# The last store of a mean kernel: one store of four partitions 32 apart that GpSimd awaits, or two stores of neighbouring pairs that SyncE and ScalarE issue and await

## The chip, the cores and the metric

The kernel runs on one core of one Trainium2 chip. The metric is the device time of one execution in microseconds (us); smaller is better. A profile's "span" is a little shorter than that time, since it ends with the program's last instruction and the runtime's closing part follows.

## The reference

```python
def setup_inputs():
    return {"x": np.random.randn(64, 256, 8192).astype(np.float32)}

def reference(x: np.ndarray) -> np.ndarray:
    return np.mean(x, axis=2)
```

That is 16384 rows of 8192 numbers, 536.87 MB, and one mean for each row.

## The kernel before

63 blocks of 256 rows are loaded by SyncE and summed by VectorE (the very last pieces shared with ScalarE). The last block is cut smaller and smaller, so that little work is left when its last piece lands. Its second half of 128 rows, one row per partition, ends in a column of 128 sums, one in each partition. A transpose on VectorE turns each group of 32 partitions by itself, so the results lie in four rows of 32 numbers, at partitions 0, 32, 64 and 96. One store takes these four rows.

```python
    def store_last(r):
        nc.vector.transpose(out=fin_t[r][:], in_=fin[r][:])
        return nc.sync.dma_start(out=out_last[r], in_=fin_t[r][0:P:SQ, :])
    # ... all loads and sums ...
    scaled_sum(fin[0][:, 0:1], head[:])
    st = store_last(0)
    # ...
    untracked(scaled_sum(fin[1][:, 0:1], fin_in[:, 0 : lastw + k]))._wait_ge(sem, 16)
    with tc.issue_after(st.ins):
        last_store = store_last(1)
```

At the end every engine reports by a drain (a semaphore counts the reports), GpSimd waits for the four reports, clears the kernel's semaphores, and awaits the last store, which no other engine waits for.

```python
    with nc.body("awaits", parent=parent, valid_engines=[SP]):
        for num, (name, count) in sems.items():
            if num != stored:
                nc.sync.wait_ge(bass.SemaphoreHandle(name, num), count)
    last_sem = bass.SemaphoreHandle(*sems[stored][:1], stored)
    with nc.body("clears", parent=parent, valid_engines=[POOL]):
        nc.gpsimd.sem_clear(range(used[0], stored))
        nc.gpsimd.wait_ge(last_sem, 16).then_inc(last_sem, -16)
```

## Time and profile before

| | before |
|---|---|
| time, median of 6 runs | 1245.95 us (1245.82 to 1246.13) |
| profiled run: time, span | 1246.58 us, 1244.7 us |
| busy: VectorE, ScalarE | 1087.0 us, 16.5 us |
| DMA engines | nine tenths or more in 39 of 40 slices |

The DMA engines set nearly the whole time, and the change touches nothing of that. The groups of instructions that it does touch stand far down on the page (line, engine, operation, output and input, count; then busy us and mean ns of one; then idle time before it and what ended it):

```profile
L60 DVE MEMSET fin<- 128x32 f32 x2 | 0.1, 85 | 0.9 <-PEq L246 0.9
...
L97 DVE STREAM_TRANSPOSE fin_t<-fin 128x32 f32<-128x32 f32 x2 | 0.4, 212 | 0.1
```

So the question is one of tenths of a microsecond behind the last load. Such a thing is read best from one fixed point. I take the end of the last transpose, called T: before it the two kernels do the same work, behind it lies all that the change moves. "+1.577" below means 1.577 us after T.

### The profile page before, as it was taken

To read this page: it belongs to the slowest core of one execution; us is meant where nothing else is said; L and a number is where in the kernel's file an instruction comes from. 1 tells how busy PE (TensorE), PEld (TensorE's weight loads), DVE (VectorE), ACT (ScalarE), POOL (GpSimd) and SP (SyncE) were. 2 spreads that over 40 slices of the span, in tenths; PEclk is the share of its full clock that TensorE was granted. 3 is DMA by queue.
4 is the path that set the end of the run, shared out by engine and by line. 5 is a ranking of instruction groups with operands and counts; after the bars stand their busy time and mean duration, and the time that the engine had idled before them with its cause. 6 is when DMAs were issued, how large, how long until landed. Compare 5 with 4: busy or idle time off the path is not lost.

```text
span 1244.7 us, 199 instructions
## 1 busy us (share of the span) xinstructions
DVE 1087.0 (87%) x78; ACT 16.5 (1%) x13; POOL 0.2 (0%) x4
## 2 busy tenths in 40 slices
DVE  2898988989889889898898988989889898898988
ACT  0000000000000000000000000000000000000004
POOL 0000000000000000000000000000000000000000
DMA  9999999999999999999999999999999999999998
GB/s 434 411 436 438 438 438 436 428 417 438 438 438 438 436 432 413 438 438 438 438 436 438 411 434 438 438 438 438 436 425 419 438 438 438 438 436 434 411 438 373
DMA packets 10241, 536.95 MB, mean 431 GB/s; under 512 B 1280, under 2 KB 1536, under 8 KB 1792
## 3 DMA queue, kind: packets, MB, share of 16 engines
q1 hardware_dynamic: 10240, 536.94, 99.8%
q14 instruction: 1, 0.01, 0.0%
HBM read 536.87 MB, written 0.07 MB: 431 GB/s over the span
## 4 chain that ended last, share of the span: by engine, by line
DMA 70%; DVE 29%; SPq 0%; issue 0%; DVEq 0%
DMA xt<-in_x_dram 70%; DVE res L80 29%; DVE fin_in L80 0%; SPq L70 0%; DVE fin_in L86 0%; DVE fin_t L97 0%; DVEq L86 0%
## 5 line engine op out<-in xcount | busy, mean ns | idle before, releaser
L80 DVE TENSOR_REDUCE res<-xt 128x2 f32<-128x16384 f32 (+1 forms) x63 | 1076.3, 17084 | 153.8 <-DMA xt<-in_x_dram 153.8
L83 ACT ACT_TABLE_LOAD x1 | 1.3, 1283 | 1181.6 <-DVE res L80 1181.6
L83 ACT ACTIVATE xt<-xt 128x8192 f32<-128x8192 f32 (+5 forms) x6 | 14.7, 2443 | 43.9 <-DMA xt<-in_x_dram 43.7
L80 DVE TENSOR_REDUCE fin_in<-xt 128x1 f32<-128x256 f32 (+3 forms) x5 | 4.9, 1005 | 0.3 <-DMA xt<-in_x_dram 0.2
L80 DVE TENSOR_REDUCE head<-xt 128x1 f32<-128x4096 f32 x1 | 4.4, 4420 | 0.7 <-DMA xt<-in_x_dram 0.7
L83 ACT ACTIVATION_READ_ACCUMULATOR xt<-xt 128x1 f32 x6 | 1.1, 186 | 0.0
L60 DVE MEMSET fin<- 128x32 f32 x2 | 0.1, 85 | 0.9 <-PEq L246 0.9
L86 DVE TENSOR_SCALAR_CACHE_REDUCE fin_in<-fin_in 128x265 f32<-128x265 f32 x1 | 0.4, 431 | 0.2 <-DVE fin_in L80 0.2
L97 DVE STREAM_TRANSPOSE fin_t<-fin 128x32 f32<-128x32 f32 x2 | 0.4, 212 | 0.1
L138 DVE TENSOR_SCALAR bulk<-res 128x126 f32<-128x126 f32 x1 | 0.2, 228 | 0.1
L86 DVE TENSOR_SCALAR_CACHE_REDUCE head<-head 128x2 f32<-128x2 f32 x1 | 0.2, 155 | 0.1
L246 POOL MEMSET const-bfloat16-1.0<- 128x1 bf16 x1 | 0.1, 101 | 0.0
L246 POOL MEMSET const-uint8-127<- 128x1 uint8 x1 | 0.1, 101 | 0.0
L246 POOL MEMSET const-float32-0.0<- 128x1 f32 x1 | 0.1, 98 | 0.2 <-issue 0.2
L246 POOL MEMSET const-float32-1.0<- 128x1 f32 x1 | 0.1, 98 | 0.0
L86 DVE DVE_READ_ACCUMULATOR fin_in<-fin_in 128x1 f32 x1 | 0.1, 84 | 0.0
L86 DVE DVE_READ_ACCUMULATOR head<-head 128x1 f32 x1 | 0.1, 83 | 0.0
## 6 DMA issues: line engine op xcount, KB each, us to landing
xt<-in_x_dram SPq DMA_DIRECT2D x1, 4096.0 KB, 31.1
xt<-in_x_dram SPq DMA_DIRECT2D x1, 2048.0 KB, 35.7
xt<-in_x_dram SPq DMA_DIRECT2D x1, 1024.0 KB, 37.7
xt<-in_x_dram SPq DMA_DIRECT2D x63, 40.8
xt<-in_x_dram SPq DMA_DIRECT2D x1, 512.0 KB, 38.5
xt<-in_x_dram SPq DMA_DIRECT2D x1, 256.0 KB, 38.7
xt<-in_x_dram SPq DMA_DIRECT2D x1, 128.0 KB, 38.6
fin_in<-in_x_dram SPq DMA_DIRECT2D x1, 128.0 KB, 38.5
```

Of the source, the lines that this page charges most:

```text
L60: nc.vector.memset(fin[r][:], 0.0)
L80: return untracked(nc.vector.tensor_reduce(out=dst, in_=src, axis=X, op=ADD))
L83: return untracked(nc.scalar.activation(out=src, in_=src, func=COPY, accum_out=dst))
L86: return nc.vector.tensor_scalar(out=src, in0=src, scalar1=inv, scalar2=None, op0=mybir.AluOpType.mult, op1=ADD, accum_out=dst,)
L97: nc.vector.transpose(out=fin_t[r][:], in_=fin[r][:])
L138: nc.vector.tensor_scalar_mul(out=bulk[:], in0=res[:], scalar1=inv)
L246: nc = _bacc.Bacc("TRN2", target_bir_lowering=False, num_devices=1)
```

## The change

Its intent is to shorten the way from T to the end: smaller stores, issued side by side, and no engine that waits for what another could await. The transpose now reads the column with a stride of zero, so that each group's 32 results stand in all of its 32 partitions. That gives the choice of partition: 31 and 32 are neighbours and belong to different groups, and so are 95 and 96.

```diff
-    fin = [pool.tile([P, SQ], F32, name=f"fin{r}") for r in range(R)]
+    fin = [pool.tile([P, 1], F32, name=f"fin{r}") for r in range(R)]
...
-    for r in range(R):
-        nc.vector.memset(fin[r][:], 0.0)
...
+        nc.vector.transpose(out=fin_t[r][:], in_=fin[r][:].to_broadcast([P, SQ]))
...
-        last_store = store_last(1)
+        for eng, q in ((nc.sync, 0), (nc.scalar, 2)):
+            p = (q + 1) * SQ - 1
+            last_stores.append(
+                eng.dma_start(out=out_last[1, q : q + 2], in_=fin_t[1][p : p + 2, :])
+            )
...
-        nc.gpsimd.sem_clear(range(used[0], stored))
-        nc.gpsimd.wait_ge(last_sem, 16).then_inc(last_sem, -16)
+        rest = [n for n in used if n not in stored]
+        while rest:
+            run = [n for k, n in enumerate(rest) if n == rest[0] + k]
+            nc.gpsimd.sem_clear(range(run[0], run[-1] + 1))
+            rest = rest[len(run) :]
+        for eng, num in zip((nc.sync, nc.scalar), stored):
+            sem = bass.SemaphoreHandle(sems[num][0], num)
+            eng.wait_ge(sem, 16).then_inc(sem, -16)
```

More of the change, by code (lines that the diff above doesn't have):

```diff
@@ L94, in scaled_sum, with turn @@
         )
-    def store_last(r):
-        nc.vector.transpose(out=fin_t[r][:], in_=fin[r][:])
-        return nc.sync.dma_start(out=out_last[r], in_=fin_t[r][0:P:SQ, :])
+    def turn(r):
+        nc.vector.transpose(out=fin_t[r][:], in_=fin[r][:].to_broadcast([P, SQ]))
     for n in range(LB):
@@ L139 @@
     nc.sync.dma_start(out=out_bulk, in_=bulk[:])
-    scaled_sum(fin[0][:, 0:1], head[:])
-    st = store_last(0)
+    scaled_sum(fin[0][:], head[:])
+    turn(0)
+    st = nc.sync.dma_start(out=out_last[0], in_=fin_t[0][0:P:SQ, :])
     with tc.issue_after(st.ins):
@@ L147 @@
         st = nc.sync.addr_align(FETCH_BLOCK, offset=0, max_nops=0)
-    untracked(scaled_sum(fin[1][:, 0:1], fin_in[:, 0 : lastw + k]))._wait_ge(sem, 16)
+    untracked(scaled_sum(fin[1][:], fin_in[:, 0 : lastw + k]))._wait_ge(sem, 16)
+    turn(1)
+    last_stores = []
     with tc.issue_after(st.ins):
-        last_store = store_last(1)
+        for eng, q in ((nc.sync, 0), (nc.scalar, 2)):
[3 more added lines that the diff above has]
+            )
     ctx.close()
@@ L208 @@
     assert exit_ins[0].engine == SP and isinstance(exit_ins[0], mybir.InstDrain)
-    stored = last_store.ins.sync_info.on_update[0].id
+    stored = [st.ins.sync_info.on_update[0].id for st in last_stores]
     used = sorted({*sems, *(s.num for s in (*load_sem, *tail_sem))})
-    assert used == list(range(used[0], stored + 1))
+    assert used == list(range(used[0], used[-1] + 1))
     with nc.body("awaits", parent=parent, valid_engines=[SP]):
         for num, (name, count) in sems.items():
-            if num != stored:
+            if num not in stored:
                 nc.sync.wait_ge(bass.SemaphoreHandle(name, num), count)
-    last_sem = bass.SemaphoreHandle(*sems[stored][:1], stored)
-    with nc.body("clears", parent=parent, valid_engines=[POOL]):
-        nc.gpsimd.sem_clear(range(used[0], stored))
-        nc.gpsimd.wait_ge(last_sem, 16).then_inc(last_sem, -16)
+    engines = [SP, POOL, mybir.EngineType.Activation]
+    with nc.body("clears", parent=parent, valid_engines=engines):
+        rest = [n for n in used if n not in stored]
[6 more added lines that the diff above has]
+            eng.wait_ge(sem, 16).then_inc(sem, -16)
     made = {b.name: b for b in blocks}
@@ L222 @@
     blocks.remove(made["clears"])
+    drain, gather = [i for i in exit_ins if i.engine == POOL][:2]
     reports = [
-        i
-        for i in exit_ins[1 : exit_ins.index(next(i for i in exit_ins if i.engine == POOL))]
-        if isinstance(i, mybir.InstDrain)
+        i for i in exit_ins[1 : exit_ins.index(drain)] if isinstance(i, mybir.InstDrain)
     ]
-    drain, gather = [i for i in exit_ins if i.engine == POOL][:2]
     end_bb.instructions = [
```

## The prediction

> **What bounds the kernel now.** I read the page first, for what fills the span.
>
> ```profile
> span 1244.7 us, 199 instructions
> ...
> DMA  9999999999999999999999999999999999999998
> ...
> HBM read 536.87 MB, written 0.07 MB: 431 GB/s over the span
> ```
>
> The DMA engines are busy in 39 of 40 slices at nine tenths or more. 536.87 MB is the whole input, read once, and 537 MB at the 438 GB/s of the full slices is 1226 us. The change adds and removes no load, so about 1242 us of the span stand outside it: everything up to the landing of the last load. Only what follows that landing is in play. So I read the chain that ended last, cut to its end (start, length, what; in us), and then the timeline of the same stretch.
>
> ```profile
> 1202.27 38.49 DMA xt<-in_x_dram
> 1240.75 0.02 issue
> 1240.78 1.45 DVE fin_in L80 x3
> 1242.23 0.03 issue
> 1242.25 0.05 DVEq L86
> 1242.30 0.07 issue
> 1242.37 0.45 DVE fin_in L86 x2
> 1242.82 0.02 issue
> 1242.84 0.21 DVE fin_t L97
> ```
>
> The view stops at the transpose, because no landing is put to the last store. The timeline has the store's issue behind it:
>
> ```profile
> 1242.84 0.21 DVE L97 STREAM_TRANSPOSE fin_t<-fin 128x32 f32<-128x32 f32 x1
> 1243.08 0.52 SPq L98 DMA_DIRECT2D out_dram<-fin_t  x1
> ```
>
> The transpose ends at 1243.05, SyncE starts the issue at 1243.08 and is done with it at 1243.60. The span ends at 1244.67. What happens in that last 1.07 us I took from the DMA shares of four small windows (columns: window, its length, busy time of DVE, ACT and POOL, clock, DMA share, GB/s):
>
> ```profile
> 1243.50:1244.20 0.70, 0.00 (x0) 0.00 (x0) 0.00 (x0) 1.00 0.00 0
> 1244.20:1244.40 0.20, 0.00 (x0) 0.00 (x0) 0.00 (x0) 1.00 0.03 3
> 1244.40:1244.70 0.30, 0.00 (x0) 0.00 (x0) 0.00 (x0) 1.00 0.00 0
> ```
>
> Nothing moves for 0.7 us, then there is a trickle, then nothing again. The trace's single records (packets, semaphore updates, and the control instructions that the page does not count) fill this in. The four 128-byte packets start at 1244.236, .251, .263 and .295 and take 0.011 us each. The store's semaphore gets one update at 1244.084 and four more at 1244.563, .574, .586 and .629. SyncE's drain, which stands behind the issue, runs 1243.815 to 1244.192. GpSimd sees the engines' reports at 1244.218, clears semaphores from 1244.299 to 1244.434, and then has nothing to do until the fourth packet's update at 1244.629; its wait executes at 1244.654 and ends the span at 1244.671.
>
> The time that counts goes on for a little: the profiled run took 1246.58 us, 1.9 us more than its span. In that stretch the records show the barrier of the runtime's closing part, one semaphore with nine updates: 1.121 and 1242.155 (engines done early), then 1245.232, .276, .299, .397, .436, .470 and .517. The update at 1245.232 is the late one, and the rest follow it at 0.02 to 0.10 us each. I take the order to be TensorE, ScalarE, GpSimd, VectorE, SyncE, and back, since the first two updates match the drains of TensorE (ended 0.888) and ScalarE (ended 1241.998). So GpSimd holds up the end, 0.561 us after its last wait.
>
> **What the Trainium skill says.** "DMA: Bandwidth & Descriptors", section "Why a DMA increments its semaphore by 16 and not by 1": a DMA uses the largest number of engines up to 16 that divides the slowest dimension; the issuing sequencer writes the missing increments itself, and each engine adds one when its data has landed. The trace agrees: four rows, one early update and four single ones. With two rows I expect one early update and two single ones on each store, and both stores on the same two engines. The same page, "Issuing engines are not separate DMA queues", says that issuing from several engines saves only the sequencer's issue time. "Perfetto Trace Analysis", section "DMA Instruction — HWDGE (DVE, Sync)", has the issuing sequencer lock a shared descriptor generator for the issue, and says that the landing of a write to HBM can be surprisingly late. The second half agrees: last packet over at 1244.306, its update at 1244.629, 0.32 us. On the lock this trace is silent, since only SyncE issues here. "Runtime: NRT & Kernel Launch", section "The ~15µs preamble/postamble breakdown", has a barrier of 44 ns per hop that passes along the engines and back; the hops here, 0.023 to 0.098 us, fit it.
>
> **The change, part by part.**
>
> 1. The two memsets of the transposes' inputs go (VectorE, 0.085 us each, at 0.9 us). The first load lands tens of us later, so they are off the path: 0. The transposes read one column with a stride of zero in place of 32 columns; they write the same 128x32 elements, so I keep 0.21 us for them: 0.
>
> 2. The last store becomes two stores of two rows each. The issue took 0.52 us for four rows. Issues of 128 rows took 0.33 to 0.43 us, so rows cost next to nothing and the rest, about 0.1 to 0.2 us, goes with the early semaphore update, which two rows need too. What halving can save is the spread of the packets: with two packets in place of four the second update of a store would come at 1244.574 instead of the fourth at 1244.629: 0.055 us, if the issue to the first packet stays at 1244.236 - 1243.080 = 1.156 us on both queues.
>
> 3. The waits move. Before, the path was: landing at 1244.629, GpSimd's wait to 1244.671, its barrier update at 1245.232. After, GpSimd ends with its clear at 1244.434. The numbering of the built program leaves one clear, since the two awaited semaphores are the two highest. If GpSimd's 0.561 us to the barrier follow the clear as they followed the wait, its update comes at 1244.995, so 0.237 us earlier.
>
> 4. Two other engines may now be the last. ScalarE waits until about 1244.60; with the 0.157 us from its drain's end to its barrier update, it arrives at 1244.76, before GpSimd. SyncE's own update came at 1245.299, one hop of 0.023 us after VectorE's, so it was already there and its time from the last instruction to the barrier is not visible. At ScalarE's 0.16 us it arrives at 1244.76 and costs nothing. At GpSimd's 0.56 us it arrives at 1245.16, and since its turn would otherwise come at 1244.995 + 0.067 = 1245.06, the gain shrinks to 0.14 us.
>
> The sum without a collision is 0.14 to 0.24 us earlier; I take 0.2. 1245.99 - 0.2 = 1245.8 us. All else, loads and sums, is as before.
>
> **The rivals.**
>
> The descriptor generator is shared, and the two issues collide. Both queues wait for the same transpose and start within a few ns of each other. If the second has to wait for the first's 0.52 us, its drain and its landing come up to 0.5 us later. GpSimd's clear waits for all drains, so it would end near 1244.43 + 0.5 = 1244.95 and reach the barrier at 1245.5: 0.27 us slower, 1246.3 us. For it speaks the skill's lock; against it, that the part of the issue which uses the generator for two rows should be far below 0.52 us. With 0.1 to 0.2 us of waiting most of the gain is eaten: 1245.9.
>
> GpSimd's 0.561 us are not its own. If that stretch is, say, a fetch of instructions that runs from some earlier event, or SyncE and ScalarE have a long way to the barrier after a semaphore wait, then moving the waits frees nothing: 1246.0, the same to 0.1 us. The barrier records give only one value per engine, so I can't rule this out.
>
> The store was never the limit at all, since other DMA traffic hides it. Against: the last window before it shows 0 GB/s and the waits for it stand at the very end. I give this nothing.
>
> **Range and chances.** The three outcomes span 1245.75 to 1246.3 us. The three runs before lie within 0.17 us of each other. The stream of loads can shift by some tenths between occasions (the profiled run was 0.6 us over the median). Range 1245.4 to 1246.4. 2% is 25 us, and the change touches about 2.5 us of the whole; so faster by over 2% gets 0.003, within 2% 0.99, slower 0.007, the last for a disturbed run.
>
> **What would show it right or wrong.** Right: 0.52 us issues on both SyncE and ScalarE, side by side at about 1243.08 us; packets on two engines only; each store's last update near 1244.57; a span shorter by 0.05 to 0.1 us, ended by a wait of SyncE or ScalarE; GpSimd's last instruction at about 1244.43 and its barrier update 0.56 us later. Step 2 fails if one of the two issues is longer than 0.6 us or its first packet comes later than 1.2 us after its start. Step 3 fails if GpSimd's barrier update stays at 0.56 us after the landing. Step 4 fails if the late barrier update is SyncE's or ScalarE's. The whole is wrong if the time rises by more than 0.4 us with the loads ending at the same point, or if the loads themselves end elsewhere, which nothing in the change explains.

## The result and the profile after

| | before | after |
|---|---|---|
| time, median of 6 runs | 1245.95 us (1245.82 to 1246.13) | 1245.37 us (1245.22 to 1245.75) |
| profiled run: time, span | 1246.58 us, 1244.7 us | 1245.66 us, 1244.0 us |

The ratio of the times is 0.9996, with a 95% interval of 0.9983 to 1.0009. A ratio here is the mean time of one kernel's runs over that of the other's of the same rounds, so it is not quite the ratio of the medians. The interval includes 1, but the six runs of one kernel don't overlap with the six of the other, and the medians are 0.58 us apart.

The page of the kernel after, cut to the lines that answer to those of before; the queue lines give packets, MB and share:

```profile
span 1244.0 us, 199 instructions
...
DMA  9999999999999999999999999999999999999998
...
q1 hardware_dynamic: 10236, 536.94, 99.8%
...
q10 hardware_dynamic: 4, 0.00, 0.0%
HBM read 536.87 MB, written 0.07 MB: 432 GB/s over the span
...
L96 DVE STREAM_TRANSPOSE fin_t<-fin 128x32 f32<-128x32 f32 x2 | 0.4, 212 | 0.1
```

The loads are as before. The memsets are gone, the transpose with the zero stride takes the same 212 ns, and a second queue, q10, carries four packets: ScalarE's two rows and their two semaphore updates.

The end of the chain that ended last (start, us, what):

```profile
1240.36 0.02 issue
1240.38 1.47 DVE fin_in L78 x3
1241.85 0.03 issue
1241.88 0.05 DVEq L84
1241.93 0.06 issue
1241.99 0.45 DVE fin_in L84 x2
1242.44 0.02 issue
1242.46 0.21 DVE fin_t L96
```

It has the same pieces with the same lengths to 0.02 us, all about 0.38 us earlier: T is 1242.674 after and 1243.052 before. That shift is no work of the change. The experiments below have their T between 1242.19 and 1242.50, whether they carry the change or not; the profile of before was just a late one (its 1246.58 us lie 0.6 us over its median). This is why I compare from T.

The timeline from the transpose on:

```profile
1242.46 0.21 DVE L96 STREAM_TRANSPOSE fin_t<-fin 128x32 f32<-128x32 f32 x1
1242.70 0.29 SPq L155 DMA_DIRECT2D out_dram<-fin_t  x1
1242.71 0.53 ACTq L155 DMA_DIRECT2D out_dram<-fin_t  x1
```

Both issues start 0.03 us after T, as the one did before. SyncE's now takes 0.29 us in place of 0.52, ScalarE's takes 0.53. The DMA shares of three small windows behind them (window, length, busy of DVE, ACT and POOL, clock, DMA share, GB/s):

```profile
1242.50:1243.40 0.90, 0.17 (x1) 0.00 (x0) 0.00 (x0) 1.00 0.03 9
1243.40:1243.60 0.20, 0.00 (x0) 0.00 (x0) 0.00 (x0) 1.00 0.03 3
1243.60:1244.10 0.50, 0.00 (x0) 0.00 (x0) 0.00 (x0) 1.00 0.00 0
```

The trickle of the rows, which came 1.18 us after T before, now comes at 1243.47, 0.80 us after T. (The 9 GB/s of the first window are one fetch of instructions.) The trace's single records give the rest. The "barrier" is the runtime's closing one, with nine updates of one semaphore; I read its order as TensorE, ScalarE, GpSimd, VectorE, SyncE and back; the last experiment below, where SyncE comes last, fits this: there the late update is the fifth, while here it is the third, as GpSimd's should be.

| from T, us | before | after |
|---|---|---|
| first packet: SyncE's store, ScalarE's store | +1.184, none | +0.797, +0.816 |
| last update of the store's semaphore: SyncE's, ScalarE's | +1.577, none | +1.131, +1.308 |
| last drain's report | +1.142 | +0.866 |
| GpSimd's clear ends | +1.382 | +1.105 |
| last wait for a store ends | +1.619 (GpSimd) | +1.346 (ScalarE) |
| barrier: ScalarE's update | long before | +1.490 |
| barrier: GpSimd's update | +2.180 | +1.633 |
| barrier over (last update) | +2.465 | +1.917 |

GpSimd's update is the late one in both, 0.284 to 0.285 us before the end of the barrier. After the change ScalarE's update comes at +1.490, and one ordinary hop to GpSimd is 0.038 us (from the second barrier of the same trace); so GpSimd is 1.633 - 1.490 - 0.038 = 0.105 us late, and the landing of the stores is no longer what sets the end. From T, the change is worth 2.465 - 1.917 = 0.548 us. A second profile of the changed kernel (the run after_again below) has the barrier over at +1.981, since ScalarE's drain reported 0.064 us later; so such records repeat to about 0.07 us. The first profile is the odd one here: of the five profiles with these two stores, the other four have the last report at +0.913 to +0.932. So the gain from T is 0.484 to 0.548 us, with the lower figure the more usual.

### The profile page after: what moved, and what is told of

It reads as the page before. It is cut to its first block, busy times and chain, and to the rows that moved or that the text cites. A ratio compares the mean times of both kernels' runs of the same rounds, so it can differ in the third digit from the quotient of the medians.

```text
span 1244.0 us, 199 instructions
## 1 busy us (share of the span) xinstructions
DVE 1086.9 (87%) x76; ACT 16.4 (1%) x13; POOL 0.2 (0%) x4
## 4 chain that ended last, share of the span: by engine, by line
DMA 70%; DVE 29%; SPq 0%; issue 0%; DVEq 0%
DMA xt<-in_x_dram 70%; DVE res L78 29%; DVE fin_in L78 0%; SPq L68 0%; DVE fin_in L84 0%; DVE fin_t L96 0%; DVEq L84 0%
```

## The experiments

My theory was that the gain has two parts: the moved waits take GpSimd's idle time off the path (and GpSimd needs some 0.53 to 0.56 us from its last instruction to the barrier), and the stores start their packets sooner. The rivals: that all came from the stores, that the number of rows and not their distance makes the issue quick, and that the two issues get in each other's way. All times are medians of 4 or 5 runs (of 2 for strided_by_scalar) beside the median of the kernel before in the same rounds; "+" numbers are from T in the one profile of that run.

| run | time, us | before there, us | barrier over |
|---|---|---|---|
| wait_by_sync | 1245.55 | 1245.94 | +2.126 |
| pairs_wait_gpsimd | 1245.77 | 1245.94 | +2.194 |
| pairs_strided | 1246.30 | 1245.94 | +2.633 |
| four_neighbours | 1245.56 | 1245.94 | +2.075 |
| both_on_sync | 1245.54 | 1246.00 | +2.091 |
| both_on_scalar | 1245.70 | 1246.00 | +2.201 |
| sync_clears | 1245.35 | 1246.00 | +1.811 |
| after_again | 1245.44 | 1246.00 | +1.981 |
| four_every_other | 1246.04 | 1245.90 | +2.579 |
| four_by_scalar | 1246.01 | 1245.90 | +2.542 |
| sync_awaits_both | 1245.12 | 1245.90 | +1.652 |
| strided_by_scalar | 1246.66 | 1245.90 | +3.209 |

### The wait part alone (wait_by_sync)

```diff
 # kernel before
-    with nc.body("clears", parent=parent, valid_engines=[POOL]):
+    with nc.body("clears", parent=parent, valid_engines=[SP, POOL]):
...
-        nc.gpsimd.wait_ge(last_sem, 16).then_inc(last_sem, -16)
+        nc.sync.wait_ge(last_sem, 16).then_inc(last_sem, -16)
```

> The wait part alone: the one store of four rows 32 partitions apart as before, awaited by SyncE, GpSimd ending with its clear. All times from the end of the last transpose (before: closing barrier's late update of GpSimd at +2.18, last update of that barrier +2.465; after: +1.63 and +1.917). Theory A (GpSimd needs about 0.53 to 0.56 us from its last instruction to its barrier update, whatever that instruction is): clear ends at +1.38 as before, GpSimd's update at about +1.93, barrier over at about +2.21, 0.25 us less than before. If SyncE too needs some 0.5 us after its wait at +1.62, the gain shrinks to about 0.13. Theory B (the gain of the change is all in the quicker issue of the stores): GpSimd's update stays near +2.18 and the time within 0.05 us of before.

Measured: 0.39 us under the kernel before, and 2.465 - 2.126 = 0.339 us from T. GpSimd's clear ends at +1.315 (SyncE's drain reported 0.066 us earlier than in the profile of before), and its barrier update comes 0.528 us later, at +1.843. SyncE's wait still ends at +1.612, as late as before, and yet the barrier passes it without a halt. So the update of GpSimd hangs on GpSimd's own last instruction, and theory B is out. With a drain as late as in the profile of before the gain would be 0.27 us. That late drain (0.377 us) is the odd one: SyncE's drain behind strided rows takes 0.310 or 0.311 us in this run, pairs_strided and four_every_other. So the moved wait alone is worth 0.27 to 0.34 us, and more likely the upper figure.

### The store part alone (pairs_wait_gpsimd)

```diff
 # kernel after
-            eng.wait_ge(sem, 16).then_inc(sem, -16)
+            nc.gpsimd.wait_ge(sem, 16).then_inc(sem, -16)
```

> The store part alone: the two pair stores of the changed kernel, both awaited by GpSimd behind its clear. Theory A: the pair landing last (ScalarE's, +1.31) ends GpSimd's wait at about +1.35, its barrier update follows 0.53 to 0.56 us later at about +1.89, barrier over at about +2.18: 0.29 us less than before, 0.26 more than the changed kernel. Theory B: the barrier is over as in the changed kernel, +1.92, all 0.55 us gained.

Measured: the waits end at +1.347, GpSimd's update comes at +1.909 and the barrier is over at +2.194, within 0.02 us of theory A. The stores alone gain 0.271 us from T (0.17 us in the medians). Over all of the runs GpSimd needs 0.527 or 0.528 us where it ends with the clear and 0.561 or 0.562 us where it ends with a wait.

### The same pairs, 32 partitions apart (pairs_strided)

```diff
 # kernel after
-            p = (q + 1) * SQ - 1
...
-                eng.dma_start(out=out_last[1, q : q + 2], in_=fin_t[1][p : p + 2, :])
+                eng.dma_start(out=out_last[1, q : q + 2], in_=fin_t[1][q * SQ : (q + 2) * SQ : SQ, :])
```

> The changed kernel with each store's two rows 32 partitions apart (0 and 32, 64 and 96) in place of neighbours; the result stays right. In the changed kernel SyncE's first packet came 0.77 us after its issue began, in the kernel before (four rows, 32 apart) 1.16 us. Theory C (the number of rows or of engines used sets that time): 0.77 us again, and a time like the changed kernel's. Theory D (the distance of the rows sets it): 1.0 to 1.16 us, GpSimd's report and clear as late as before, time 0.3 to 0.4 us over the changed kernel's.

The timeline of this run:

```profile
1242.39 0.52 SPq L154 DMA_DIRECT2D out_dram<-fin_t  x1
1242.39 1.34 ACTq L154 DMA_DIRECT2D out_dram<-fin_t  x1
```

SyncE's issue takes 0.52 us for two rows, as it did for four, and its first packet comes at +1.180 as before. So the distance of the rows makes the issue long and not their number: theory D. ScalarE's issue takes 1.34 us, which neither theory had. With it the drains report at +1.582, and the time is 0.36 us over the kernel before, so more above the changed kernel than even theory D had. Two queues with strided rows lose.

### One store of four neighbours (four_neighbours)

```diff
 # kernel before; wrong results on purpose
-        return nc.sync.dma_start(out=out_last[r], in_=fin_t[r][0:P:SQ, :])
+        src = fin_t[r][SQ - 1 : SQ + 3, :] if r else fin_t[r][0:P:SQ, :]
+        return nc.sync.dma_start(out=out_last[r], in_=src)
```

> The kernel before, the last store taken from the four neighbouring partitions 31 to 34 (one queue, awaited by GpSimd as before; the last 128 results are wrong on purpose, shape and bytes are the same). Theory C (number of rows): issue to first packet 1.16 us and 0.52 us of issue as before, same time as before. Theory D (distance of the rows): first packet at about 0.77 us, issue about 0.3 us, landing 0.35 us earlier and the time 0.35 us under the kernel before.

From its timeline:

```profile
1242.34 0.30 SPq L99 DMA_DIRECT2D out_dram<-fin_t  x1
```

0.30 us for four rows that are neighbours, against 0.52 us for four that are 32 apart; the first packet at +0.815, the last landing at +1.188, and a time 0.38 us under the kernel before. Theory D again, within 0.04 us. One store of four neighbours would even land 0.12 us before the second of two pairs (+1.308). It can't be had from this transpose: four partitions side by side hold two groups at most.

### Every other partition (four_every_other)

```diff
 # kernel before; wrong results on purpose
-        return nc.sync.dma_start(out=out_last[r], in_=fin_t[r][0:P:SQ, :])
+        src = fin_t[r][SQ - 1 : SQ + 7 : 2, :] if r else fin_t[r][0:P:SQ, :]
+        return nc.sync.dma_start(out=out_last[r], in_=src)
```

> The kernel before, its last store taken from partitions 31, 33, 35 and 37 (wrong results on purpose). Four neighbours gave an issue of 0.305 us and a first packet 0.787 us after its start; four rows 32 apart gave 0.521 and 1.156 us. If only direct neighbours are quick: 0.52 and 1.15 us here, time as before. If the distance counts, or there is a limit between 2 and 32: 0.31 and 0.79 us, and some 0.35 us under the kernel before.

```profile
1242.34 0.63 SPq L99 DMA_DIRECT2D out_dram<-fin_t  x1
```

0.63 us, a first packet at +1.305 and a time 0.14 us over the kernel before. A distance of 2 is no better than one of 32. Of the steps tried (1, 2 and 32) only the step of one partition is quick, and since these four rows start at the same partition 31 as the four neighbours, it is not the place of the first row. Why, the runs do not show.

### One queue for both pairs (both_on_sync, both_on_scalar)

```diff
 # kernel after
-        for eng, q in ((nc.sync, 0), (nc.scalar, 2)):
+        for eng, q in ((nc.sync, 0), (nc.sync, 2)):      # both_on_sync
+        for eng, q in ((nc.scalar, 0), (nc.scalar, 2)):  # both_on_scalar
```

> Both pair stores issued by SyncE, one after the other; awaited by SyncE and ScalarE as in the changed kernel. If the second queue is what helps: the second issue starts about 0.35 us after the first, its last landing comes at about +1.45 to +1.5 from the end of the transpose (changed kernel +1.31), SyncE's drain ends about 0.2 us later than the changed kernel's last drain (+0.86), and the time is 0.15 to 0.25 us over the changed kernel's. If the two queues only get in each other's way (one descriptor generator, same two engines): within 0.05 us of the changed kernel.

> Both pair stores issued by ScalarE. In the changed kernel ScalarE's issue took 0.533 us beside SyncE's 0.289 us. Theory E (the two issues share a generator and ScalarE's waits for SyncE's): here the first issue of ScalarE, with none beside it, takes about 0.29 us. Theory F (ScalarE's issue is slower by itself): 0.53 us again. Landing of the second pair later than +1.31 either way, time 0.1 to 0.3 us over the changed kernel's.

On SyncE the issues take 0.289 and 0.246 us one after the other (0.60 us with the gap), the second pair lands at +1.500, and the barrier is over at +2.091, 0.11 us after the +1.981 of after_again; in the medians it is 0.10 us. So the second queue is worth about 0.1 us, a little less than I expected, because GpSimd's clear and not the landing sets the end. On ScalarE the first issue takes 0.535 us with nothing beside it, just as beside SyncE's. That is theory F: in the changed kernel the two issues show no sign of disturbing each other. The time is 0.26 us over after_again, inside what both theories had. ScalarE's second issue takes 0.247 us, like SyncE's, so it is the first one that costs it more. That one is ScalarE's first issue in the whole program, while SyncE had made 72 before its own; whether this or the engine is the reason was not tried.

These two runs also show when a landing comes late. From the first packet to the last update of its semaphore it is 0.337 and 0.336 us for the two pairs on SyncE and 0.336 and 0.334 us on ScalarE, but 0.492 us for ScalarE's pair in the changed kernel, whose packets come 0.02 us behind SyncE's. The Trainium skill ("DMA: Bandwidth & Descriptors", section "Queues, rings and completion order") says that a semaphore update lands only after every earlier write of that DMA engine, across its queues. A late landing would point that way if both pairs use the same two engines, as the prediction took from that page. But the records that I have do not name the engine of a packet, and the rule alone does not give the size: SyncE's updates were out by +1.131, and with 0.336 us ScalarE's last would have come at about +1.15, not at +1.308. So the cause of the late landing stays open.

### Is the extra time of strided rows on ScalarE a collision? (four_by_scalar, strided_by_scalar)

```diff
 # four_by_scalar: kernel before
-        return nc.sync.dma_start(out=out_last[r], in_=fin_t[r][0:P:SQ, :])
+        eng = nc.scalar if r else nc.sync
+        return eng.dma_start(out=out_last[r], in_=fin_t[r][0:P:SQ, :])
 # strided_by_scalar: pairs_strided
-        for eng, q in ((nc.sync, 0), (nc.scalar, 2)):
+        for eng, q in ((nc.scalar, 0), (nc.scalar, 2)):
```

> The kernel before, its last store (four rows 32 apart) issued by ScalarE with no other store beside it. In the run with two strided pairs ScalarE's issue took 1.344 us and its first packet came 1.505 us after its start, beside SyncE's 0.515 us issue. If that was a wait for the shared generator: about 0.75 to 0.8 us here (SyncE's 0.521 plus the 0.25 us by which ScalarE's issue of a pair is longer), first packet at about 1.2 us. If ScalarE's strided issue is that slow by itself: 1.3 us and 1.5 us here too.

```profile
1242.39 1.08 ACTq L99 DMA_DIRECT2D out_dram<-fin_t  x1
```

1.08 us fits neither number, and lies between them: most of the slowness is ScalarE's own, and 0.27 us were left to explain. So I ran the strided pairs on ScalarE alone:

> Both strided pairs issued by ScalarE, none by SyncE. ScalarE's issue of a strided pair took 1.344 us beside SyncE's 0.515 us issue, its issue of four strided rows alone 1.078 us. If the 0.27 us between them are a wait for a generator shared with SyncE: the first issue here takes about 1.08 us and its first packet comes about 1.24 us after its start. If a strided pair is just that slow on ScalarE: 1.34 us and 1.5 us.

The records give 1.065 us for the first issue and a first packet 1.226 us after its start. The pair alone is as slow as the four rows alone, so the other 1.344 - 1.065 = 0.28 us came with SyncE's issue beside it. (One profile stands for each side, and the rows differ: 64 and 96 there, 0 and 32 here.) Two issues can collide then, as the rival said, but only strided ones do here; the neighbouring pairs do not (0.533 beside SyncE, 0.535 alone).

### Taking GpSimd out of the end (sync_clears, after_again)

```diff
 # kernel after
+        nc.sync.wait_ge(told, 4).then_inc(told, -4)      # the gathering of the reports
...
-            nc.gpsimd.sem_clear(range(run[0], run[-1] + 1))
+            nc.sync.sem_clear(range(run[0], run[-1] + 1))
...
-        *made["awaits"].instructions, *reports, drain, gather, *made["clears"].instructions
+        *made["awaits"].instructions, *reports, drain, *made["clears"].instructions
```

> The changed kernel with the gathering of the reports and the clear done by SyncE in the time in which it waits for its store; GpSimd does nothing at the end. Theory A (GpSimd's 0.53 us from clear to barrier is its own and sets the end of the changed kernel): the barrier's second update is now free to follow ScalarE's (+1.49) by one hop of 0.04 us, the barrier is over at about +1.81 in place of +1.92, 0.1 us less. Rival: ScalarE's and SyncE's own way to the barrier already holds it up, or SyncE becomes the last: no gain, or a loss of 0.1 us or more.

> The changed kernel once more, beside the others on the same chip. Its records should repeat to 0.05 us from the end of the transpose: SyncE's issue 0.29 us, ScalarE's 0.53 us, last landing +1.31, GpSimd's barrier update +1.63, barrier over +1.92; time 0.4 to 0.65 us under the kernel before. If SyncE and ScalarE race for the generator, the roles may be swapped: ScalarE 0.29 us and SyncE 0.53 us.

The barrier is over at +1.811, as theory A had it (+1.81); GpSimd's update follows ScalarE's (+1.489) by 0.038 us. So GpSimd's way from its clear to the barrier did set the end of the changed kernel, by 0.106 us against the first profile of it and 0.170 us against after_again. The medians, 1245.35 and 1245.44, are closer than that and their runs overlap; in time alone this step would not be proven. after_again repeats the issues (0.288 and 0.535 us), the last landing (+1.308) and the gain in time (0.56 us); GpSimd's update (+1.697) and the end of the barrier came 0.064 us later than in the first profile, which is more than the 0.05 us that I had allowed.

### A version that beats both (sync_awaits_both)

```diff
 # sync_clears
-    with nc.body("clears", parent=parent, valid_engines=[SP, mybir.EngineType.Activation]):
+    with nc.body("clears", parent=parent, valid_engines=[SP]):
...
-            eng.wait_ge(sem, 16).then_inc(sem, -16)
+            nc.sync.wait_ge(sem, 16).then_inc(sem, -16)
```

> Built on the run in which SyncE clears: SyncE, last in the barrier's order, also awaits ScalarE's store. From the end of the last transpose: ScalarE's landing stays at +1.31, SyncE's second wait ends near +1.35. If SyncE reaches the barrier some 0.15 us after its last wait, as ScalarE does, its update comes at +1.50 in place of +1.595 and the barrier is over at about +1.71 in place of +1.81: 0.1 us less, about 0.7 us under the kernel before. If SyncE needs 0.25 us or more, no gain.

```profile
span 1243.5 us, 199 instructions
```

The span is 1.13 us shorter than that of before by the records, of which 1243.05 - 1242.19 = 0.86 us is the earlier T. The rest, 0.28 us, is the earlier end of the last wait (+1.343 in place of +1.619). ScalarE now ends with its drain and is at the barrier at +1.077. SyncE, which stands last in the order, awaits both stores to +1.343 and gives its update at +1.489, 0.146 us later. The three hops that used to follow ScalarE's late update are now run through early (SyncE's update came at +1.595 in sync_clears, 0.106 us later), and the barrier is over at +1.652, earlier than the +1.71 that I expected. The difference is the hop behind SyncE's update, 0.044 us here and 0.097 or 0.098 us in the other profiles; why is open. The time is 1245.12 us (1244.91 to 1245.25), 0.78 us under the kernel before in the same rounds, where the changed kernel had 0.58 and 0.56. The two were not run in the same rounds, and not on the same chip.

## Why the prediction was right or wrong

The class was right, but it says nothing of the argument: the loads fill the time, and the change touches some 2.5 us of 1246. The direction was right as well, but the gain was 0.58 us where I had put 0.2, nearly three times as much, and the median of 1245.37 us lies 0.03 us below the lower end of my range. Point by point:

**Step 1** (memsets and transpose cost nothing) held: 212 ns for the transpose, before and after.

**Step 2** is the term that was mis-sized. I let the pairs save only the spread of their packets, 0.055 us, "if the issue to the first packet stays at 1.156 us". It did not stay: it fell to 0.768 us, because the rows are neighbours. I had read that the number of rows costs next to nothing, which is right (two strided rows take 0.515 us, four 0.521), and overlooked that "neighbouring" could matter at all; every issue in the trace of before had either all 128 partitions or four of them 32 apart, so the trace had set the two cases side by side and I put the difference down to the early semaphore update. The runs put it in the step: 0.30 us for four neighbours, which make the same early update. The updates themselves came as expected, one early and two single ones for each store. What the quicker issue did was more than the landing. In all fourteen profiles the drain behind a last store ends 0.106 to 0.108 us after that store's early semaphore update, and this update comes sooner with neighbours: at +0.644 (SyncE) and +0.751 (ScalarE) in place of +1.032. So the last report came at +0.866 in place of +1.142, and GpSimd's clear came sooner by as much. These 0.276 us set a late drain against an early one; with wait_by_sync's +1.076 and after_again's +0.930 it is 0.146 us. I had left the reports where they were.

**Step 3** was right in mechanism and near in size. GpSimd ended with its clear, and its way to the barrier followed it: 0.528 us where I had taken over 0.561. Alone (wait_by_sync) the step brought 0.339 us, or 0.27 us with the late drain of before, where I wrote 0.237.

How the two parts go together can be read from four kernels, by the end of the barrier: +2.465 with neither, +2.126 with the moved wait alone, +2.194 with the pairs alone, +1.917 and +1.981 with both. While GpSimd still waits for the stores, the path runs through the last landing, and the pairs bring 0.271 us. With the wait moved, it runs through the last report and GpSimd's clear, and they bring 0.145 to 0.209 us. From T the parts alone sum to 0.610 us, against 0.484 to 0.548 us for both; in the medians they sum to 0.39 + 0.17 = 0.56 us, against 0.58 and 0.56. With a spread of 0.07 us and more, the runs do not tell how far the parts overlap.

**Step 4** held in the form that I thought best: ScalarE takes 0.144 us from its last wait to the barrier (0.145 to 0.156 us in the other profiles where it ends with a wait) and SyncE, in sync_awaits_both, 0.146 us, so neither became the last.

**The rivals.** The collision on the descriptor generator was absent in the changed kernel and is real with strided rows, 0.28 us. The rival that GpSimd's half microsecond is not its own fell with wait_by_sync and sync_clears; what fills it, the records do not show. Of the signs that I named, the landings of both stores "near 1244.57" (+1.52) failed, as they came at +1.131 and +1.308, and so did 0.52 us for SyncE's issue. From T the span became 0.273 us shorter (+1.346 in place of +1.619), not 0.05 to 0.1 us, and GpSimd's last instruction ended at +1.105, not at about +1.38. ScalarE's issue, 0.533 us, and the end of the span by ScalarE's wait held; on which engines the packets ran, the records do not say.

## What to carry to other kernels

When a kernel is bound by its loads, its end is still a chain of its own, and it can be read to less than 0.1 us if all records are counted from one point that the change doesn't touch; the times alone, which spread by 0.3 to 0.5 us here, would not have told these parts apart. For a small store that stands at the very end, try to take the rows from partitions side by side, even if that costs a trick to place them, and look at what else waits for that store's issue, as the reporting drains do here. And ask which engine closes the program last: here it paid to keep GpSimd out of the end and to let the engine that is asked last do the waiting.

## What the Trainium skill lacked or had wrong

- "DMA: Bandwidth & Descriptors" does not say that the step between partitions sets how long a small store's issue takes: 0.289 us (two rows) and 0.305 us (four) for direct neighbours on SyncE, 0.515 and 0.521 us at a step of 32, 0.632 us at a step of 2. Its 0.6 us to the first byte for these queues, of which it does not say where the count starts, was not reached by the last store in any of the runs: from the start of the issue to the first packet it was 0.77 to 1.28 us on SyncE and 0.74 to 1.51 us on ScalarE.
- "DMA: Bandwidth & Descriptors" says that issuing from several engines saves only the sequencer's time. Neither that page nor another says that ScalarE's first issue takes longer than SyncE's: 0.535 us against 0.289 for a neighbouring pair, 1.065 against 0.515 us for a strided one. Its second takes 0.247 us and 0.490 us. (SyncE had issued 72 times before.)
- "Perfetto Trace Analysis" has the issuing engines share one locked generator. With neighbouring pairs no run shows a wait (0.533 us beside SyncE, 0.535 us alone); with strided pairs ScalarE's issue grew from 1.065 to 1.344 us.
- "Runtime: NRT & Kernel Launch" gives 44 ns per hop of the barrier, and as a mean of eight hops that is right: the second barrier of the closing part took 0.355 to 0.358 us in all fourteen profiles. Single hops were 0.023 to 0.098 us. It does not have what each engine needs from its last instruction to the barrier: GpSimd 0.527 to 0.562 us, ScalarE 0.144 to 0.159 and SyncE 0.146 us.
- No page that I read has what a drain behind a small store waits for: it ended 0.106 to 0.108 us after the store's early semaphore update, whether the issue took 0.25 or 1.34 us.
- No page that I read has the time of a clear of a range of semaphores (17 here) by engine: 0.135 us on GpSimd, 0.055 us on SyncE.
